# Unmasked decays in a hybrid SSD and attention block: the mask moves to the product of C and B, and the third pair's projections go between the convolution tiles

## The chip, the cores and the metric

The kernel runs on one core of a Trainium2 chip, in fp32 throughout (a matmul operand is split into a high and a low part, and three matmuls make one product). The metric is the device time of one execution, the median of several runs, in microseconds (us). Five engines take part, each with its own queue of instructions that it works through in order: PE (TensorE), DVE (VectorE), ACT (ScalarE), POOL (GpSimd) and SP (SyncE, which issues most DMAs here).

## The reference, cut to what matters

The block mixes a Mamba-2 SSD group (8 heads) and a stick-breaking attention group (8 heads, in 4 pairs), joins them by an output projection with normalization, and adds a gated feed-forward part. The change touches the SSD group and the order of the projections:

```python
proj = h @ w_in                                  # z, xbc, dt_raw, q, k, v
xbc = silu(causal_depthwise_conv(xbc, conv_w, conv_b))   # x, B and C of the SSD
a_cs = cumsum(dt * a)                            # per head
decay_in = exp(segsum(adt))                      # exp(a_cs[l] - a_cs[s]) where l >= s, else 0
cb = einsum("bclgn,bcsgn->bgcls", cc, bc)        # C times B, per group of 4 heads
y_diag = einsum("bgcls,bgrcls,bcsgrp->bclgrp", cb, decay_in, x)
```

Only the product of `cb`, `decay_in` and the mask counts, so the mask may stand on any factor. `a` is negative, so the difference is at most 0 wherever the mask keeps it.

## The kernel before, in words

The sequence of 1024 is cut into 8 blocks of 128. The front of the kernel normalizes and splits the input and projects q, k and v of the first pair of heads (q0, k0, v0). `dt_stage` then computes the time steps and their running sum `acs`, writes it to DRAM, and reads it back broadcast to all partitions, one tile `ab` (128 x 8 heads x 128, 512 KB) for each block. For each block it masks `ab` on POOL (an affine_select that puts -1e30 above the diagonal, L360), subtracts `acs` on DVE (one tensor_tensor over 8 heads, L361), takes the exponential on ACT (L362), and stores the decays to DRAM by a DMA that POOL issues (L363). The tiles `ab` borrow the buffers of the attention (`sp`, `sn`) and of the SSD (`u`, `dec`). Behind the last exponential ACT makes the scales `msc` that the attention's sigmoids need.

Then two streams are woven into one by `merge`. One is the attention: for each unit of a pair, a head and a query block, `weigh` makes scores on PE (`zp`, L565 and L566), two sigmoids on ACT (`sn` L567, `sp` L568), a select on POOL (L570), a running product on DVE (the scan, L571) and a product (L572); `turn` transposes the weights on PE (`tp`, L582) and splits them (`wh` on ACT, `wl` on DVE, L587); `mix_v` multiplies by v (`o`, L594). The other is the filling work, in the order of the table `PLAN`: `qkv1` (projections of the second pair), `x0` to `x7` (projections of xbc with their convolutions, whose taps on DVE, L384, are taken up as side work), `qkv2`, the SSD, `qkv3`, and the gates `z0` to `z3`. Every projection is made in two halves of 512 columns (`pj_q`, `pj_k`, `pj_v`, `pj_x`: 24 matmuls each, L78 to L80) in two PSUM banks, and each half is read out by DVE (`kr` L278, `vr` L284, `u` L375) before its bank can be used again. `merge` counts the PE time that the filling has issued and the DVE time that the attention has issued, and lets the attention go on while its share is below a curve through the nine values of `PACE`; so the table `PACE` sets when the attention starts and how fast it goes beside the filling. What comes out is one fixed order for each engine.

In the SSD, `front` makes for one block the products of C and B on PE (`pcb`, L420), multiplies them into the decays that are read back from DRAM (`Gm`, L427), and `ssd` multiplies `Gm` by the inputs on PE (`py`, L445). A front is issued one step ahead of the `py` that uses it.

After the last gate come the output projection and the feed-forward part, which is more than half of the time.

Of the kernel before, what the change touches and what calls it, by code (L numbers as in the profile page):

```python
# [33 lines left out]
NEG = -1e30  # L34

PLAN = ('qkv1', 'x0', 'x1', 'x2', 'x3', 'x4', 'x5', 'qkv2', 'x7', 'x6', 'ssd', 'qkv3', 'z0', 'z1', 'r0', 'z2', 'z3', 'wo', 'l1', 'o0')

PACE = (-0.109, 0.104, 0.264, 0.337, 0.474, 0.601, 0.751, 0.876, 1.027)
# [10 lines left out]
def tile_hybrid_block(  # L49
# [126 lines left out]
    ORDER = [f"{k}{t[3]}" if t[:3] == "qkv" else t for t in PLAN if t[0] in "qxz" for k in ("qkv" if t[0] == "q" else "x")]  # L176
# [83 lines left out]
    def qkv_tiles(j, st):  # L260
# [15 lines left out]
        def evac_k(n, ps, sl):  # L276
            kr = t2.tile([P, 512], F32, tag="t2", name="kr")
            V.tensor_tensor(kr, ps, R_b[:, sl], ALU.mult)  # L278
            two("k", n, kr)
            st["k"] = n == 1  # L280
# [13 lines left out]
    v_first = []  # L294

    def proj_qkv(j, st):
        for key, evac in zip("qkv", qkv_tiles(j, st)):
            yield from proj(f"{key}{j}", evac, {"q": 0.6, "k": 1.2, "v": 0.6}[key])


    def dt_stage():
# [50 lines left out]
        yield  # L352
        for b in range(NB):
# [6 lines left out]
            G.affine_select(ab, ab, [[0, NH], [-1, P]], ALU.is_ge, NEG, base=0, channel_multiplier=1)  # L360
            V.tensor_tensor(ab, ab, acs[:, b, :, None].to_broadcast([P, NH, P]), ALU.subtract)  # L361
            last = A.activation(ab, ab, AF.Exp)  # L362
            G.dma_start(dec_d[b], ab.rearrange("p h l -> p (h l)"))  # L363

        with tc.issue_after(last.ins):
            A.activation(rqp, rs, AF.Copy, scale=0.125)
            A.activation(rqn, rs, AF.Copy, scale=-0.125)

# [40 lines left out]
    def ssd():  # L409
        state = None  # L410

        def front(b):
# [8 lines left out]
            for g in range(2):  # L421
                T.transpose(pcb[:, 2 + g, :], cx[:, 4 + g, :], ident)
            bs = sml.tile([P, 2, P], F32, tag="bs", name="bs", bufs=2)
            A.copy(bs, pcb[:, 2:4, :])
            Gm = big.tile([P, NH, P], F32, tag="G", name="Gm")
            for g in range(2):
                V.tensor_tensor(  # L427
                    Gm[:, 4 * g : 4 * g + 4, :], de[:, 4 * g : 4 * g + 4, :],
                    pcb[:, g, None, :].to_broadcast([P, 4, P]), ALU.mult,
                )  # L430
# [173 lines left out]
    def attention(st):  # L604
# [6 lines left out]
        def ready(j):  # L611
            while "v" not in st[j]:
                yield 0, 0
# [92 lines left out]
    for _ in dts:  # L706
        pass
# [99 lines left out]
    def stage(t):  # L807
        nonlocal wo
        if t[:3] == "qkv":
            yield from proj_qkv(int(t[3]), st[int(t[3])])  # L810
        elif t[0] == "x":
# [609 lines left out]
```

## Time and profile before

| | |
|---|---|
| time, median of 3 runs | 1226.1 us (1224.39 to 1229.47) |
| time of the profiled execution | 1223.84 us |
| span of the profiled execution, first to last instruction | 1222.1 us |
| PE busy | 1186.1 us, 97% of the span |
| DVE busy | 929.8 us, 76% |
| ACT busy | 585.3 us, 48% |
| POOL busy | 92.6 us, 8% |
| mean granted clock of PE | 0.997 of full speed |

A row of the timeline gives the start, the duration, the engine, the line, the operation, what is written and read, the shapes and a count; behind it in brackets stand the engine's idle time before it and what ended that time. Rows of one line that follow each other are merged under one count. On PE and DVE an instruction begins before the one ahead of it has quite ended, so that the distance of two starts, and not a duration, is what an instruction costs in a dense stretch. In a table by stages the busy time of each engine stands with the number of its instructions behind it; what is missing to the length of the stage is idle time.

### The profile page before, as it was taken

The page shows a single profiled execution, that of the slowest core. Times are in us where ns is not written, and L with a number is a line of the kernel's source. Part 1 is how long each engine was busy: PE and PEld are TensorE (multiplying, and loading weights), DVE is VectorE, ACT ScalarE, POOL GpSimd, SP SyncE. Part 2 cuts the span into 40 slices and gives each one's busy share as a digit, 9 for nine tenths or more (in the row PEclk, how much of TensorE's full clock was granted, in tenths as well). Part 3 has the DMA queues.
Part 4 walks back from the last instruction along what each step waited for, and adds up shares of the span by engine and source line. Part 5 has one row for each costly group of instructions (what it writes and reads, how often), then busy time and mean ns, then how long its engine had stood idle before and what let it go on. Part 6 is the DMA issues. An engine that isn't in the chain of part 4 may idle for free.

```text
span 1222.1 us, 16315 instructions
## 1 busy us (share of the span) xinstructions
PE 1186.1 (97%) x5641; PEld 966.0 (79%) x5641; DVE 929.8 (76%) x1461; ACT 585.3 (48%) x1115; POOL 92.6 (8%) x232
## 2 busy tenths in 40 slices
PE   9998999999999998999999999999999999999997
PEld 7776778887887776788788888888888888888885
DVE  7478988769997978668898755566555558998877
ACT  7347655546654776446653323333233335444453
POOL 0041110010100100011200000000000000000000
PEclk9999999999999999999999999999999999999999
DMA  6793342345657424767973322322223298233346
GB/s 192 198 341 111 92 134 91 118 118 172 180 151 221 137 79 155 227 191 221 314 207 110 104 77 79 104 69 87 78 78 104 96 334 285 69 122 100 114 136 236
DMA packets 141994, 184.27 MB, mean 151 GB/s; under 512 B 10724, under 2 KB 96964, under 8 KB 141912
## 3 DMA queue, kind: packets, MB, share of 16 engines
q1 hardware_dynamic: 130656, 152.23, 40.8%
q0 software_dynamic: 7424, 25.17, 5.5%
q10 hardware_dynamic: 3832, 5.84, 1.3%
q8 instruction: 44, 0.72, 0.3%
q14 instruction: 38, 0.31, 0.1%
HBM read 133.28 MB, written 49.92 MB: 150 GB/s over the span
## 4 chain that ended last, share of the span: by engine, by line
PE 72%; DVE 13%; DMA 5%; ACT 5%; issue 4%; SPq 1%; DVEq 0%; ACTq 0%
PE pd L79 5%; PE pd L78 5%; PE pd L80 5%; DVE sn L571 3%; DMA Rb<-r_d 2%; PE o L594 2%; PE tp L582 2%; PE pj_x L78 2%; PE pj_x L80 2%; PE pcu L80 2%; PE pcg L80 2%; PE peu L80 2%; PE peg L80 2%; PE peu L79 2%; PE peg L79 2%
## 5 line engine op out<-in xcount | busy, mean ns | idle before, releaser
L74 ACT CAST flhi<-fraw 128x512 fp32r<-128x512 f32 x98 | 60.3, 621 | 153.5 <-PE pcg L79 35.6
L79 PE MATMUL pd<-folo,fohi 128*128 128x512 f32 x260 | 101.4, 390 | 0.0
L80 PE MATMUL pd<-fohi,folo 128*128 128x512 f32 x260 | 101.2, 389 | 0.0
L78 PE MATMUL pd<-fohi 128*128 128x512 f32 x260 | 101.2, 389 | 0.0
L571 DVE TENSOR_TENSOR_SCAN sn<-sn,smask 128x1024 f32<-128x1024 f32 (+3 forms) x64 | 87.3, 1365 | 17.6 <-ACT sn L567 17.4
L75 DVE TENSOR_TENSOR fllo<-fraw,flhi 128x512 fp32r<-128x512 f32 x98 | 66.7, 684 | 29.2 <-ACT flhi L74 29.2
L567 ACT ACTIVATE sn<-zp,msc 128x512 f32<-128x512 f32 (+2 forms) x96 | 56.0, 585 | 34.5 <-PE zp L566 28.9
L74 ACT CAST fohi<-rt 128x512 fp32r<-128x512 f32 x83 | 48.5, 618 | 45.6 <-PE pd L79 22.9
L586 ACT CAST wh<-tp 128x512 fp32r<-128x512 f32 (+1 forms) x80 | 42.7, 544 | 38.5 <-PE tp L582 38.0
L74 ACT CAST flhi<-fs 128x512 fp32r<-128x512 f32 x44 | 27.3, 622 | 69.5 <-PE peg L79 34.5
L75 DVE TENSOR_TENSOR folo<-rt,fohi 128x512 fp32r<-128x512 f32 x83 | 54.9, 687 | 7.3 <-ACT fohi L74 7.3
L587 DVE TENSOR_TENSOR wl<-tp,wh 128x512 fp32r<-128x512 f32 (+1 forms) x80 | 49.7, 628 | 10.8 <-ACT wh L586 10.3
L79 PEld LDWEIGHTS pd<-folo,fohi 128*128 128x128 f32 x260 | 48.8, 188 | 10.6 <-DVE folo L75 0.6
L568 ACT ACTIVATE sp<-zp,msc 128x512 f32<-128x512 f32 (+2 forms) x96 | 55.9, 585 | 2.5 <-PE tp L582 2.4
L78 PEld LDWEIGHTS pd<-fohi 128*128 128x128 f32 x260 | 48.8, 188 | 10.2
L80 PEld LDWEIGHTS pd<-fohi,folo 128*128 128x128 f32 x260 | 48.8, 188 | 10.1
L582 PE MATMUL tp<-ident,sp 128*128 128x128 f32 x288 | 48.0, 278 | 5.7 <-DVE sp L572 5.1
L78 PE MATMUL po<-woh,yhl 128*128 128x512 f32 x128 | 50.5, 395 | 2.6 <-ACT yhl L74 2.2
L1015 POOL DMA_DIRECT2D a_d<-sg x44 | 23.9, 542 | 376.8 <-DVE sg L1014 376.8
L78 PE MATMUL pj_x<-hh,wh_x 128*128 128x512 f32 x128 | 52.2, 408 | 0.0
L80 PE MATMUL pj_x<-hh,wl_x 128*128 128x512 f32 x128 | 51.0, 398 | 0.0
L80 PE MATMUL po<-woh,yhl 128*128 128x512 f32 x128 | 50.1, 393 | 0.5 <-DVE yhl L75 0.5
(425 smaller groups left out, 3457.6 us busy)
## 6 DMA issues: line engine op xcount, KB each, us to landing
ps<-a_d SPq DMA_DIRECT2D x55, 256.0 KB
fraw<-in_w_gate_dram SPq DMA_DIRECT2D x22, 512.0 KB
fraw<-in_w_up_dram SPq DMA_DIRECT2D x22, 512.0 KB
a_d<-sg POOLq DMA_DIRECT2D x44, 256.0 KB, 2.6
rt<-in_w_down_dram SPq DMA_DIRECT2D x33, 256.0 KB
rt<-a_d SPq DMA_DIRECT2D x22, 256.0 KB
ps<-in_w_down_dram SPq DMA_DIRECT2D x22, 256.0 KB
xt<-in_x_t_dram SPq DMA_DIRECT2D x8, 512.0 KB
```

The source lines that it names most:

```text
L74: A.copy(hi, src)
L75: V.tensor_tensor(lo, src, f32(hi), ALU.subtract)
L78: T.matmul(ps, lhsT=ah, rhs=bh, start=start, stop=False, skip_group_check=more)
L79: T.matmul(ps, lhsT=ah, rhs=bl, start=False, stop=False, skip_group_check=more)
L80: last_mm[0] = T.matmul(ps, lhsT=al, rhs=bh, start=False, stop=stop, skip_group_check=more)
L567: A.activation(sn[:, 1 + off : 1 + off + cw_], zp[:, 0:cw_], AF.Sigmoid, scale=rqn[:, qb : qb + 1])
L568: A.activation(sp[:, off : off + cw_], zp[:, 0:cw_], AF.Sigmoid, scale=rqp[:, qb : qb + 1])
L571: V.tensor_tensor_scan(sn[:, 1 : 1 + W], sn[:, 1 : 1 + W], smask[:, 0:W], 1.0, ALU.mult, ALU.max)
L582: T.transpose(tp[:, P * i : P * i + P], ws[a][:, co : co + P], ident)
L586: A.copy(wh[:, 0:n_], tp[:, 0:n_])
L587: V.tensor_tensor(wl[:, 0:n_], tp[:, 0:n_], f32(wh[:, 0:n_]), ALU.subtract)
L594: T.matmul(o[:, 0:cw_], lhsT=vv[:, k, h, :], rhs=wt[:, c0 : c0 + cw_], start=(first and k == kb + 1 and wt is wh), stop=(last and k == kb ...
```

## The change

The decays lose their mask: the affine_select on `ab` goes, and DVE subtracts `acs` with 64 tensor_scalar instructions (one for each block and head, 128 columns, subtract and then a minimum with 0) where 8 tensor_tensor instructions (1024 columns) stood. The mask is put on C times B instead: ACT copies the 256 columns of `pcb` to SBUF (`cb`), POOL masks them by an affine_select, and DVE multiplies the decays by `cb` rather than by PSUM.

The work on the 8 blocks is no longer issued in one piece ahead of the two streams. All 8 loads are still issued first; the rest becomes side work of the filling, one block at a time: three blocks at once, four after DVE has been given the first half of k1, and the last after the second half. The attention may begin its first unit only when all of this has been issued.

In `PLAN` the one entry `qkv2` becomes `q2`, `k2` and `v2` between x tiles, and the first five values of `PACE` are lower.

```diff
-PLAN = ('qkv1', 'x0', 'x1', 'x2', 'x3', 'x4', 'x5', 'qkv2', 'x7', 'x6', 'ssd', 'qkv3', 'z0', 'z1', 'r0', 'z2', 'z3', 'wo', 'l1', 'o0')
-PACE = (-0.109, 0.104, 0.264, 0.337, 0.474, 0.601, 0.751, 0.876, 1.027)
+PLAN = ('qkv1', 'x0', 'q2', 'x1', 'x2', 'k2', 'x3', 'x4', 'v2', 'x5', 'x7', 'x6', 'ssd', 'qkv3', 'z0', 'z1', 'r0', 'z2', 'z3', 'wo', 'l1', 'o0')
+PACE = (-0.14, 0.06, 0.195, 0.33, 0.465, 0.601, 0.751, 0.876, 1.027)
...
         def evac_k(n, ps, sl):
             kr = t2.tile([P, 512], F32, tag="t2", name="kr")
-            V.tensor_tensor(kr, ps, R_b[:, sl], ALU.mult)
+            i = V.tensor_tensor(kr, ps, R_b[:, sl], ALU.mult)
+            if j == 1:
+                k_evac.append(i)
...
+        abs_ = []
         for b in range(NB):
...
-            G.affine_select(ab, ab, [[0, NH], [-1, P]], ALU.is_ge, NEG, base=0, channel_multiplier=1)
-            V.tensor_tensor(ab, ab, acs[:, b, :, None].to_broadcast([P, NH, P]), ALU.subtract)
+            abs_.append(ab)
+        for b, ab in enumerate(abs_):
+
+            while len(k_evac) < (0, 1, 2)[(b > 2) + (b > 6)]:
+                yield 0, 0
+
+            with tc.issue_after(k_evac[-1].ins) if k_evac else nullcontext():
+                for h in range(NH):
+                    V.tensor_scalar(ab[:, h, :], ab[:, h, :], acs[:, b, h : h + 1], 0.0, ALU.subtract, ALU.min)
             last = A.activation(ab, ab, AF.Exp)
             G.dma_start(dec_d[b], ab.rearrange("p h l -> p (h l)"))
+            yield 0, 1.7
...
+        decayed.append(True)
...
+            cb = sml.tile([P, 2, P], F32, tag="cb", name="cb")
+            A.copy(cb, pcb[:, 0:2, :])
+            G.affine_select(cb, cb, [[0, 2], [-1, P]], ALU.is_ge, 0.0, base=0, channel_multiplier=1)
...
                 V.tensor_tensor(
                     Gm[:, 4 * g : 4 * g + 4, :], de[:, 4 * g : 4 * g + 4, :],
-                    pcb[:, g, None, :].to_broadcast([P, 4, P]), ALU.mult,
+                    cb[:, g, None, :].to_broadcast([P, 4, P]), ALU.mult,
                 )
...
-            while "v" not in st[j]:
+            while "v" not in st[j] or not decayed:
                 yield 0, 0
...
-    for _ in dts:
-        pass
+    for _ in range(4):
+        next(dts)
+    side.append(dts)
```

The order on DVE at the decays, before. `ab` is the tile of one block's decays, `kr` and `kl` belong to the second pair's k, whose two halves stand in the PSUM tiles `pj_k`; `ql` and `wl_v` are low parts of q1 and of the weights of v1, and `vv` is the first pair's v.

```order
L75 TENSOR_TENSOR wl_v_827<-wr_v_824,wh_v_826 128x512
L361 TENSOR_TENSOR ab<-ab,acs 128x1024
L75 TENSOR_TENSOR ql<-pj_q_768,qh 128x512
L361 TENSOR_TENSOR ab<-ab,acs 128x1024 x2
L278 TENSOR_TENSOR kr<-pj_k_799,R_b 128x512
L75 TENSOR_TENSOR kl<-kr,kh 128x512
L361 TENSOR_TENSOR ab<-ab,acs 128x1024 x4
L278 TENSOR_TENSOR kr<-pj_k_844,R_b 128x512
L550 TENSOR_TENSOR vv_925<-pv,vv_925 128x8x64
L75 TENSOR_TENSOR kl<-kr,kh 128x512
```

The same place on DVE after the change:

```order
L371 TENSOR_SCALAR ab<-ab,acs 128x128 x8
L74 TENSOR_TENSOR ql<-pj_q_748,qh 128x512
L371 TENSOR_SCALAR ab<-ab,acs 128x128 x16
L74 TENSOR_TENSOR wl_v_807<-wr_v_804,wh_v_806 128x512
L277 TENSOR_TENSOR kr<-pj_k_779,R_b 128x512
L371 TENSOR_SCALAR ab<-ab,acs 128x128 x4
L74 TENSOR_TENSOR kl<-kr,kh 128x512
L371 TENSOR_SCALAR ab<-ab,acs 128x128 x28
L277 TENSOR_TENSOR kr<-pj_k_834,R_b 128x512
L371 TENSOR_SCALAR ab<-ab,acs 128x128 x6
L74 TENSOR_TENSOR kl<-kr,kh 128x512
L371 TENSOR_SCALAR ab<-ab,acs 128x128 x2
```

Before, seven blocks stood ahead of the second half's `kr` and the eighth came some rows further down; now 56 of the 64 instructions stand ahead of it, and the last 8 right behind it.

The order on ACT between the last exponentials and the attention's first sigmoids, before. `wh_x` is the high part of the weights of x0, which a DMA loads.

```order
L362 ACTIVATE ab<-ab 128x1024
L74 CAST kh<-kr 128x512
L549 CAST vv_925<-pv 128x8x64
L74 CAST wh_x_949<-wr_x_947 128x512
L74 CAST wh_x_986<-wr_x_984 128x512
L362 ACTIVATE ab<-ab 128x1024
L366 ACTIVATE msc<-msc 128x8
L367 ACTIVATE msc<-msc 128x8
L567 ACT_TABLE_LOAD
L567 ACTIVATE sn<-zp,msc 128x512
L568 ACTIVATE sp<-zp,msc 128x512
```

And after:

```order
L372 ACTIVATE ab<-ab 128x1024 x4
L73 CAST kh<-kr 128x512
L73 CAST wh_x_924<-wr_x_922 128x512
L372 ACTIVATE ab<-ab 128x1024
L377 ACTIVATE msc<-msc 128x8
L378 ACTIVATE msc<-msc 128x8
L73 CAST wh_x_961<-wr_x_959 128x512
L582 ACT_TABLE_LOAD
L582 ACTIVATE sn<-zp,msc 128x512
L583 ACTIVATE sp<-zp,msc 128x512
```

One of the two casts of x0's weights still stands ahead of the last exponential, the other now behind it; the readout of `vv` has moved behind the first sigmoids.

The order on PE at the first block of the SSD (block 7), before. `pxs` are transposes of the inputs, `pj_k` belongs to the fourth pair.

```order
L422 MATMUL pcb<-ident,cx 128x128 x2
L433 MATMUL pxs<-ident,cx 128x128 x4
L582 MATMUL tp<-ident,sp 128x128 x4
L80 MATMUL pj_k_3244<-hh_0_187,wl_k_2967 128x512
L78 MATMUL pj_k_3244<-hh_0_189,wh_k_2966 128x512
L79 MATMUL pj_k_3244<-hl_0_190,wh_k_2966 128x512
L565 MATMUL zp<-kh,qq 128x512
L566 MATMUL zp<-kl,qq 128x512
L594 MATMUL o<-wh,vv_2898 128x256
L80 MATMUL pj_k_3244<-hh_0_189,wl_k_2967 128x512
L565 MATMUL zp<-kh,qq 128x384
L445 MATMUL py<-xdt,Gm 128x64 x8
```

And after:

```order
L434 MATMUL pcb<-ident,cx 128x128 x2
L448 MATMUL pxs<-ident,cx 128x128 x4
L597 MATMUL tp<-ident,sp 128x128 x8
L77 MATMUL pj_k_3282<-hh_0_195,wh_k_3011 128x512
L609 MATMUL o<-wh,vv_2937 128x256
L78 MATMUL pj_k_3282<-hl_0_196,wh_k_3011 128x512
L460 MATMUL py<-xdt,Gm 128x64 x4
L79 MATMUL pj_k_3282<-hh_0_195,wl_k_3012 128x512
L460 MATMUL py<-xdt,Gm 128x64 x4
```

The first `py` stands behind fewer matmuls than before, and there are now a copy and a select between `pcb` and the `Gm` that `py` reads.

Behind the gates z0 to z3 every engine has the same order as before.

## Rows read from the trace of the kernel before

**Rows 1.** The page's first part: busy time, share of the span and number of instructions of each engine.

```profile
PE 1186.1 (97%) x5641; PEld 966.0 (79%) x5641; DVE 929.8 (76%) x1461; ACT 585.3 (48%) x1115; POOL 92.6 (8%) x232
```

**Rows 2.** The table by stages: start and end of a stage, its length, then busy time and number of instructions of PE, weight loads, DVE, ACT and POOL, PE's granted clock, the DMA engines' busy share and GB/s.

```profile
85.60:94.40 8.80, 7.20 (x30) 5.28 (x29) 7.65 (x9) 4.77 (x8) 2.98 (x8) 1.00 1.02 365
94.40:110.00 15.60, 10.97 (x52) 8.43 (x53) 11.14 (x10) 12.65 (x25) 2.35 (x8) 0.89 0.32 100
110.00:150.00 40.00, 36.91 (x204) 30.25 (x203) 38.71 (x52) 27.17 (x51) 5.15 (x19) 1.00 0.36 93
150.00:200.00 50.00, 47.81 (x241) 38.45 (x240) 44.45 (x53) 27.68 (x47) 5.51 (x17) 1.00 0.40 116
200.00:250.00 50.00, 48.56 (x254) 40.96 (x254) 39.42 (x51) 27.71 (x51) 4.62 (x18) 1.00 0.39 118
250.00:300.00 50.00, 49.06 (x251) 39.33 (x250) 39.81 (x49) 29.96 (x54) 5.31 (x15) 1.00 0.42 120
300.00:405.00 105.00, 103.00 (x647) 87.26 (x648) 93.74 (x148) 58.35 (x134) 10.30 (x40) 1.00 0.62 184
```

**Rows 3.** Who PE waited for from 80 to 110 us: the waiting instruction, what ended the wait, us in total, times, the longest.

```profile
PE zp L565 <- ACT sp L568: 3.5, 1, 3.5
PE pj_v L78 <- DVE kr L278: 1.6, 1, 1.6
PE tp L582 <- DVE sp L572: 0.6, 1, 0.6
PE o L594 <- DVE wl L587: 0.5, 1, 0.5
```

**Rows 4.** The timeline of PE: two matmuls of k1 in a dense stretch, the transposes of the first pair's v, the two long waits, and two matmuls behind the second.

```profile
67.25 0.39 PE L78 MATMUL pj_k<-hh,wh_k 128*128 128x512 f32 x1
67.48 0.39 PE L79 MATMUL pj_k<-hl,wh_k 128*128 128x512 f32 x1
...
80.48 1.03 PE L548 MATMUL pv<-ident,vr 128*128 128x128 f32 x8
...
87.22 0.50 PE L78 MATMUL pj_v<-hh,wh_v 128*128 128x512 f32 x1 [1.58 <-DVE kr L278]
...
97.90 0.50 PE L565 MATMUL zp<-kh,qq 128*128 128x512 f32 x1 [3.52 <-ACT sp L568]
...
100.06 0.63 PE L78 MATMUL pj_x<-hh,wh_x 128*128 128x512 f32 x1
100.49 0.63 PE L79 MATMUL pj_x<-hl,wh_x 128*128 128x512 f32 x1
```

**Rows 5.** The timeline of DVE at the decays and at the attention's first weights.

```profile
75.24 0.68 DVE L278 TENSOR_TENSOR kr<-pj_k,R_b 128x512 f32<-128x512 f32 x1
76.95 5.07 DVE L75 TENSOR_TENSOR kl<-kr,kh 128x512 fp32r<-128x512 f32 x1 [1.03 <-ACT kh L74]
81.95 4.62 DVE L361 TENSOR_TENSOR ab<-ab,acs 128x1024 f32<-128x1024 f32 x4
86.49 0.68 DVE L278 TENSOR_TENSOR kr<-pj_k,R_b 128x512 f32<-128x512 f32 x1
...
92.77 1.21 DVE L361 TENSOR_TENSOR ab<-ab,acs 128x1024 f32<-128x1024 f32 x1
...
100.96 1.22 DVE L572 TENSOR_TENSOR sp<-sp,sn 128x1024 f32<-128x1024 f32 x1 [0.20 <-POOL sp L570]
...
104.32 1.09 DVE L572 TENSOR_TENSOR sp<-sp,sn 128x896 f32<-128x896 f32 x1 [0.20 <-ACT sp L568]
```

**Rows 6.** The timeline of POOL at the decays.

```profile
77.25 4.22 POOL L360 TENSOR_SCALAR_AFFINE_SELECT ab<-ab 128x1024 f32<-128x1024 f32 x4
...
88.78 1.11 POOL L360 TENSOR_SCALAR_AFFINE_SELECT ab<-ab 128x1024 f32<-128x1024 f32 x1
```

**Rows 7.** The timeline of ACT from the casts of x0's weights to the first sigmoids.

```profile
88.84 1.15 ACT L74 CAST wh_x<-wr_x 128x512 fp32r<-128x512 f32 x2
94.01 1.06 ACT L362 ACTIVATE ab<-ab 128x1024 f32<-128x1024 f32 x1 [4.03 <-DVE ab L361]
...
95.28 1.28 ACT L567 ACT_TABLE_LOAD   x1
96.58 0.69 ACT L567 ACTIVATE sn<-zp,msc 128x512 f32<-128x512 f32 x1
97.17 0.68 ACT L568 ACTIVATE sp<-zp,msc 128x512 f32<-128x512 f32 x1
```

**Rows 8.** The timeline of SP: the issue of the two loads of x0's weights (start, us, count).

```profile
82.42 1.18 SPq L168 DMA_DIRECT2D wr_x<-in_w_in_dram  x2
```

**Rows 9.** Groups of DVE by line and shape (count, busy us, mean ns of one, idle us before): 128 columns of SBUF with two tensors, and with one tensor and two constants.

```profile
L755 DVE TENSOR_TENSOR rt<-rt 36x128 f32<-36x128 f32 x2 | 0.6, 283 | 0.2
...
L757 DVE TENSOR_SCALAR rt<-rt 36x128 f32<-36x128 f32 x2 | 0.4, 216 | 0.0
```

**Rows 10.** The copy of the second half of `pcb` on ACT, as a group of the same kind.

```profile
L424 ACT COPY bs<-pcb 128x256 f32<-128x256 f32 x8 | 3.0, 378 | 3.2 <-PE pcb L422 3.2
```

**Rows 11.** Selects of 128 columns on POOL, as groups of the same kind: the attention's, and one at the kernel's start.

```profile
L570 POOL TENSOR_SCALAR_AFFINE_SELECT sp<-sp 128x128 f32<-128x128 f32 x64 | 32.0, 501 | 182.2 <-ACT sp L568 180.9 <-PE zp L565 1.1
...
L111 POOL TENSOR_SCALAR_AFFINE_SELECT tri<-ones_f 128x128 f32<-128x128 f32 x1 | 0.3, 290 | 0.0
```

**Rows 12.** The view of line 363, the stores of the decays that POOL issues: from issue to landing, us.

```profile
DMA to landing us min/median/max: 4.2/5.2/7.7
```

More of the change, by code (lines that the diff above doesn't have):

```diff
@@ L33 @@
 EPS = 1e-6
-NEG = -1e30
-PLAN = ('qkv1', 'x0', 'x1', 'x2', 'x3', 'x4', 'x5', 'qkv2', 'x7', 'x6', 'ssd', 'qkv3', 'z0', 'z1', 'r0', 'z2', 'z3', 'wo', 'l1', 'o0')
-PACE = (-0.109, 0.104, 0.264, 0.337, 0.474, 0.601, 0.751, 0.876, 1.027)
+PLAN = ('qkv1', 'x0', 'q2', 'x1', 'x2', 'k2', 'x3', 'x4', 'v2', 'x5', 'x7', 'x6', 'ssd', 'qkv3', 'z0', 'z1', 'r0', 'z2', 'z3', 'wo', 'l1', 'o0')
+PACE = (-0.14, 0.06, 0.195, 0.33, 0.465, 0.601, 0.751, 0.876, 1.027)
 A_ALL, F_ALL = 146.4, 259.0
@@ L172, in load_w_half @@
         return hi, lo
-    ORDER = [f"{k}{t[3]}" if t[:3] == "qkv" else t for t in PLAN if t[0] in "qxz" for k in ("qkv" if t[0] == "q" else "x")]
+    ORDER = [f"{k}{t[3]}" if t[:3] == "qkv" else t for t in PLAN if t[0] in "qkvxz" for k in ("qkv" if t[:3] == "qkv" else "x")]
     START = {"q": COL_Q, "k": COL_K, "v": COL_V, "x": COL_XBC, "z": COL_Z}
@@ L292, in qkv_tiles, with proj_qkv @@
         return evac_q, evac_k, evac_v
-    v_first = []
-    def proj_qkv(j, st):
+    v_first, k_evac, decayed = [], [], []
+    def proj_qkv(j, st, keys="qkv"):
         for key, evac in zip("qkv", qkv_tiles(j, st)):
-            yield from proj(f"{key}{j}", evac, {"q": 0.6, "k": 1.2, "v": 0.6}[key])
+            if key in keys:
+                yield from proj(f"{key}{j}", evac, {"q": 0.6, "k": 1.2, "v": 0.6}[key])
     def dt_stage():
@@ L810, in stage @@
             yield from proj_qkv(int(t[3]), st[int(t[3])])
+        elif t[0] in "qkv":
+            yield from proj_qkv(int(t[1]), st[int(t[1])], t[0])
         elif t[0] == "x":
```

## The prediction

> **What bounds the kernel now.** I read the page's first part, then the table by stages, then who PE waited for in the stage where it stood still longest, then the timelines of the engines that it waited for. PE is busy for 97% of the span [rows 1], so an edit is worth the time in which PE waits because of it, and nothing beyond that. Behind the gates the order of every engine stays, so what is won or lost is settled between the decays and the gates. The stages show where there is something to win [rows 2]: PE stands still for 1.60 us from 85.6 to 94.4 us and for 4.63 us from 94.4 to 110, and in the second of these its granted clock is 0.89. From 110 to 200 us it is idle for 3.09 + 2.19 = 5.28 us while DVE is busy for 83.16 of 90 us (92%); from 200 to 300 us for 1.44 + 0.94 = 2.38 us while DVE is busy for 79.23 of 100 (79%).
>
> Four waits make the idle time of 80 to 110 us [rows 3]. The long ones are 1.58 us for a PSUM bank of k1 that DVE had not read out (`kr`), and 3.52 us for a score bank that ACT's first sigmoids had not read out [rows 4]. Behind the second, matmuls of 512 columns come 0.43 us apart instead of 0.23 [rows 4]: the lower of PE's two clocks, 1.2 instead of 2.4 GHz. Over that stage it costs (1 - 0.89) x 15.6 = 1.7 us [rows 2]. Behind the wait of 1.58 us the granted clock stayed at 1.00 [rows 2].
>
> Both long waits come from the decays. DVE's `kl` took 5.07 us [rows 5], where the next subtraction of twice its size takes 1.21, and it covers POOL's four selects, 4.22 us from 77.25 [rows 6]: DVE was held while POOL masked. Four subtractions follow (4.62 us), and only then `kr` at 86.49 [rows 5]. The eighth block's select comes at 88.78 [rows 6], its subtraction at 92.77 [rows 5], its exponential at 94.01, then the load of a table and the first sigmoids, which end at 97.85 [rows 7]; PE goes on at 97.90 [rows 4].
>
> **The change part by part.**
>
> *The selects on POOL go.* That frees DVE of some 5.07 - 0.68 = 4.4 us of being held at `kl` (the 0.68 is `kr`, of the same size) and takes a step out of the chain of each block.
>
> *64 small subtractions for 8 large ones.* The nearest row is a tensor_scalar of 128 columns, 216 ns, against 283 for a tensor_tensor of that size [rows 9]. In a dense row an instruction costs less than its duration: four subtractions take 4.62 us, one alone 1.21, so the distance is (4.62 - 1.21) / 3 = 1.14, or 0.07 less. So 64 cost between 64 x 0.14 = 9.0 and 64 x 0.216 = 13.8 us, against 8 x 1.14 = 9.1 before. Alone that would be 0 to +4.7 us on DVE; with the 4.4 us of holding gone it is -4.5 to +0.3.
>
> *The wait for `kr`.* In the new order `kl` and 28 subtractions (3.9 to 6.0 us) stand between the two halves. With `kl` starting at 76.95 as before, the second `kr` starts at 81.5 to 83.7. PE wanted its bank at 87.22 - 1.58 = 85.64 [rows 4]. The wait goes, with 2 us to spare or more: -1.58.
>
> *The wait for the sigmoids.* Behind `kr` come the last 8 subtractions and `kl`, 0.68 + 0.68 + 1.1 to 1.7 us: the last block is ready for its exponential at 84.0 to 86.8. On ACT a cast of x0's weights now stands ahead of that exponential. Their load was issued at 82.42 [rows 8] and cast at 88.84 [rows 7], so it takes 6.4 us at most in this crowded stage; it now stands behind `kl`'s store, can go out near 78, and is there by 84.4, so the cast is covered by DVE's end or nearly so. From the start of the exponential to the end of the first pair of sigmoids were 97.85 - 94.01 = 3.84 us; the other cast adds 0.6 [rows 7]: the score bank is free at 88.5 to 91.2. PE comes to that bank later in its order than before: the second half of v1 and 6 of the 8 transposes of the first pair's v stand ahead of it. It reaches v1's second half at 85.64 - 0.8 = 84.8 (the transposes, 1.03 us with the last one's tail, have moved behind), and then needs 12 x 0.227 + 0.7 = 3.4 us: 88.2. Wait: 0.3 to 3.0 us. I take 1.3, near the middle: -2.2.
>
> *What is late next.* The first weights need about 102.2 - 97.9 = 4.3 us from there to the end of their product on DVE, and the second ones 3.2 more (104.32 + 1.09) [rows 5]. In the new order, its matmuls counted and taken at the dense distance, PE has some 3.1 us of other work before the first transposes and some 2.2 before the second ones. That makes two waits of about 1 us, where 0.6 and 0.5 stood [rows 3]: +0.9, with 0.5 to 3.5 us of new waits as its ends (-0.6 to +2.4).
>
> *The clock.* If no wait is longer than 1.58 us, the granted clock stays at full as it did behind that one: -1.7. With a wait of 3 us it falls as before: 0.
>
> *q2, k2 and v2 between x tiles.* The x tiles carry the taps, so DVE's load is uneven [rows 2]: 92% with the tiles x0 to x4, 79% where q2, k2 and v2 stood. Mixed, it is 162.4 / 190 = 85%. PE's idle time was 0.059 us for each us in the first and 0.024 in the second. At the lower rate throughout, 7.7 us become 4.5: -3.1 at best. At the mean of both rates nothing is won; and PLAN and PACE reorder every engine, which may cost as much as 1 us. Waits pile up where an engine is almost full, so I take the value nearer to the better end: -2.0.
>
> *The mask in the SSD.* For each of 8 blocks ACT copies 256 columns (0.378 us by the same form [rows 10]) and POOL selects 256 columns: above the 0.29 us of one of 128 columns at the kernel's start, and near the mean of 0.50 of the attention's [rows 11]. No engine is full by that (ACT's 8 x 0.38 = 3 us in 105 us where it is busy for 58 [rows 2]). What counts is the chain from `pcb` to `py`: +0.9 us. In the order the first block has about 2 us of other matmuls to cover it, the later ones more than 4. So one block shows it: +0.5, ends 0 and +4.
>
> Sum: -1.58 - 2.2 + 0.9 - 1.7 - 2.0 + 0.5 = -6.1 us. The profiled execution took 1223.84 us (1.7 us outside its span); it would take 1217.7. It lies 2.3 us under the median of the runs, 1226.1, against which the forecast is made: **1220.0 us**.
>
> **The rivals.**
>
> *The wait moves and stays.* The cast ahead of the last exponential waits for its load, or the subtractions cost 216 ns each: PE waits 3 us at the score bank, the clock falls as before. Then -1.58 - 0.5 + 0.9 + 0 - 1.0 + 0.5 = -1.7: 1224.4. For it: DMA engines at a share of 1.02 [rows 2]. Against it: the load goes out 4 us earlier.
>
> *Everything comes out well.* No wait at the score bank, new waits of 0.5 us, the mix at its best: -1.58 - 3.5 - 0.6 - 1.7 - 3.1 + 0 = -10.5: 1215.6.
>
> *POOL's stores are held by DVE.* POOL was seen to hold DVE; the reverse, in the new form, no row shows. If each store can be issued only when an unbroken row of subtractions ends, the seventh block's goes out up to 1.7 us later, lands 5.2 us after that [rows 12], and a memset of POOL behind it holds the attention's first select. The first two waits at the weights grow by about 1 us each: -4.1, 1222.0. The Trainium skill, "SBUF — State Buffer", section "SBUF: two separate sides", says why it might: a DMA issued by GpSimd needs descriptors that GpSimd writes, and it cannot write them while DVE runs an operation that takes both ports, such as a one-tensor fp32 operation in SBUF. Before, DVE used two-tensor operations there and the stores landed in 4.2 to 7.7 us, so the trace does not decide it.
>
> *Slower: the mask in the SSD.* PE works in order, and `py` waits for `Gm`, which now waits for ACT, whose queue may hold 0.6 us of other work, and for POOL, which DVE can hold to about 0.6. With the copy that is 0.38 + 0.6 + 0.6 = 1.6 us for each block. If it shows on all 8, it costs 12.6 us against the 6.6 won elsewhere: +6.0, 1232.1. The sign turns at a little over 4 blocks exposed. For it: DVE is 89% busy in that stage [rows 2], and its queue holds `Gm`, so it waits too. Against it: the matmuls between `pcb` and `py` in the new order, from the second block on.
>
> **How the numbers follow.** Forecast 0.46, with its own range from 1217 to 1223; everything well 0.22; the wait moves 0.14; POOL's stores 0.06; the SSD 0.12. What a measurement can tell from no change is about 0.5%, 6.1 us here, so 1220.0 is the border. Faster: half of the forecast and all of "well", 0.45. Slower: the SSD, 0.12. Same: the rest, 0.43. The range takes the best case less 2 us and the moved wait plus the 3.4 us by which one run lay above the median: 1213 to 1228; it leaves out the SSD and a little below.
>
> **What would show it.** In the new profile: no row of DVE at the decays longer than 1.3 us, and tensor_scalar rows of 0.14 to 0.22 us; the second `kr` before 84 us and no wait of `pj_v` for it; the first sigmoid at 87 to 90 us instead of 96.58; a granted clock of 1.00 from 90 to 110 us; PE's idle time from 110 to 300 us under 6 us; no wait of `py` longer than 1 us but at the first block. The prediction is wrong if PE still waits over 2.5 us for a sigmoid, if the waits at the weights behind it come to over 3.5 us, if DVE falls behind in the mixed stretch, or if `py` waits at block after block.

## The result and the profile after

The changed kernel took 1228.62 us in the median of 20 runs, the kernel before 1226.18 us in 20 runs beside them: a ratio of 1.0022, with a 95% interval of 1.0012 to 1.0031. It is slower by about 2.4 us, where I had forecast 1220.0 us and a range of 1213 to 1228. One of the 20 executions took 4202 us and, like one each in experiments 4 and 5, is left out of the ratio, though not of the median. The profiled execution of after has a span of 1227.3 us, against 1222.1 before. These 5.2 us say little of the price of the change: the granted clock, averaged over a run, was 0.994 in the runs of both kernels, but 0.993 in the profile of after and 0.997 in that of before, which was one of its better ones. PE's idle time over the whole span is the same, 1227.3 - 1191.6 = 35.7 us after and 1222.1 - 1186.1 = 36.0 before; what differs is PE's busy time.

The page's first part, after, beside [rows 1]: PE is as full as before, and no engine has much more to do.

```profile
PE 1191.6 (97%) x5641; PEld 967.8 (79%) x5641; DVE 927.6 (76%) x1517; ACT 588.3 (48%) x1123; POOL 86.6 (7%) x232
```

The table by stages, after, with the columns of [rows 2]. PE's idle time (length less busy) is 4.41 us from 85.6 to 94.4, where it was 1.60, and 0.89 in the next stage, where it was 4.63. The clock is 0.97 and 0.91 there. From 110 to 300 us it is 6.47 us (before 7.65), but it has moved: 2.26 in the first 90 us (before 5.28) and 4.21 in the next 100 (before 2.38). From 300 to 405, where the SSD is, it is 3.56 (before 2.00). Together, from 85.6 to 405 us, it is about 0.5 us less than before.

```profile
85.60:94.40 8.80, 4.39 (x23) 3.48 (x22) 2.75 (x4) 6.38 (x11) 0.73 (x3) 0.97 1.06 378
94.40:110.00 15.60, 14.71 (x75) 12.02 (x74) 15.14 (x17) 9.84 (x20) 2.62 (x8) 0.91 0.37 110
110.00:150.00 40.00, 39.21 (x204) 32.20 (x204) 32.21 (x42) 22.42 (x42) 3.80 (x16) 1.00 0.41 112
150.00:200.00 50.00, 48.53 (x246) 38.21 (x245) 41.94 (x53) 30.77 (x55) 4.67 (x18) 1.00 0.43 126
200.00:250.00 50.00, 48.07 (x258) 40.15 (x257) 42.05 (x54) 28.14 (x50) 4.62 (x18) 1.00 0.36 95
250.00:300.00 50.00, 47.72 (x242) 37.66 (x242) 44.84 (x53) 31.30 (x55) 4.40 (x17) 1.00 0.41 111
300.00:405.00 105.00, 101.44 (x622) 83.30 (x621) 88.93 (x142) 58.05 (x138) 16.63 (x45) 1.00 0.60 176
```

Who PE waited for from 80 to 110 us, after, beside [rows 3]: the wait for `kr` is gone; the wait for the sigmoids is still there, and is longer.

```profile
PE zp L580 <- ACT sp L583: 4.4, 1, 4.4
PE o L609 <- DVE wl L602: 0.6, 1, 0.6
PE tp L597 <- DVE sp L587: 0.3, 1, 0.3
```

The timeline of DVE, after, beside [rows 5]: `kl` is back at 0.68 us, the second `kr` starts at 82.62 instead of 86.49, and the last subtraction ends at 85.47. A subtraction costs 5.59 / 28 = 0.20 us, so the 64 take 12.8 us.

```profile
76.53 0.68 DVE L74 TENSOR_TENSOR kl<-kr,kh 128x512 fp32r<-128x512 f32 x1
77.13 5.59 DVE L371 TENSOR_SCALAR ab<-ab,acs 128x128 f32<-128x128 f32 x28
82.62 0.68 DVE L277 TENSOR_TENSOR kr<-pj_k,R_b 128x512 f32<-128x512 f32 x1
...
85.00 0.47 DVE L371 TENSOR_SCALAR ab<-ab,acs 128x128 f32<-128x128 f32 x2
```

The timeline of ACT, after, beside [rows 7]: the last block is ready at 85.47, but its exponential starts at 87.51. The cast ahead of it waited 2.65 us for the load of x0's weights, and the second cast 1.01 us more. So the first sigmoid starts at 91.70.

```profile
86.98 0.62 ACT L73 CAST wh_x<-wr_x 128x512 fp32r<-128x512 f32 x1 [2.65 <-DMA wr_x<-in_w_in_dram]
87.51 1.05 ACT L372 ACTIVATE ab<-ab 128x1024 f32<-128x1024 f32 x1
...
89.77 0.62 ACT L73 CAST wh_x<-wr_x 128x512 fp32r<-128x512 f32 x1 [1.01 <-DMA wr_x<-in_w_in_dram]
90.40 1.28 ACT L582 ACT_TABLE_LOAD   x1
91.70 0.69 ACT L582 ACTIVATE sn<-zp,msc 128x512 f32<-128x512 f32 x1
```

The timeline of SP, after, beside [rows 8]: these loads were issued at 77.74, 4.7 us earlier than before, as I had worked out. The cast of the first starts 9.2 us behind the first issue.

```profile
77.74 1.92 SPq L167 DMA_DIRECT2D wr_x<-in_w_in_dram  x2
```

Behind the gates, where the order is the same, the output projection (`po`) waits for `yhl`, the high part of its input that ACT casts: the longest such wait is 3.3 us after and 1.4 before (the first row is after, the second before).

```profile
PE po L77 <- ACT yhl L73: 3.3, 1, 3.3
PE po L78 <- ACT yhl L74: 2.2, 2, 1.4
```

From 510 to 520 us, in the columns of [rows 2], PE has no idle time in either kernel, but 39 matmuls fall into this stage after, at a granted clock of 0.83, and 46 before, at 1.00. After, the clock also falls to 0.66 from 485 to 490 us, where it is 1.00 before.

```profile
510.00:520.00 10.00, 10.00 (x39) 8.05 (x38) 7.82 (x22) 6.38 (x21) 0.55 (x1) 0.83 0.75 223
510.00:520.00 10.00, 10.00 (x46) 8.29 (x45) 8.64 (x25) 4.89 (x18) 1.08 (x2) 1.00 0.71 215
```

The view of the DMA engines from 70 to 96 us, after, in 40 slices and as a sum: 26 us at 391 GB/s, the engines busy in every slice. POOL's queue (q0), which holds the stores of the decays, has 3.70 MB of it.

```profile
DMA  9999999999999999999999999999999999999999
...
DMA packets 5181, 10.17 MB, mean 391 GB/s; under 512 B 418, under 2 KB 2445, under 8 KB 5178
...
q0 software_dynamic: 1014, 3.70, 35.3%
```

The timeline of POOL, after, in place of [rows 6]: a store is issued in 0.5 to 0.8 us, but a memset of the attention's `sn` stands behind the third and waits 5.93 us until an earlier store has landed; four stores then go out in a row.

```profile
76.02 0.59 POOL L373 DMA_DIRECT2D dec_d<-ab  x1 [0.99 <-ACT ab L372]
82.55 0.10 POOL L574 MEMSET sn<- 128x1 f32 x1 [5.93 <-DMA dec_d<-ab]
83.03 2.16 POOL L373 DMA_DIRECT2D dec_d<-ab  x4 [0.39 <-issue]
```

The new select in the SSD, after, as the view of its line (duration least, median, most; first and last start), beside [rows 11], with what DVE waited for it, us and times. Its copy on ACT takes 0.374 us in the median.

```profile
L437 POOL TENSOR_SCALAR_AFFINE_SELECT cb<-cb x8: 408/408/1930, 309.0 to 402.7; 128x256 f32<-128x256 f32 x8
...
  DVE Gm L442: 1.0, 4
```

### The profile page after: what moved, and what is told of

It is laid out like the page before. It is cut to its first block, busy times and chain, and to the rows that moved or that the text cites. A ratio compares the mean times of both kernels' runs of the same rounds, so it can differ in the third digit from the quotient of the medians.

```text
span 1227.3 us, 16366 instructions
## 1 busy us (share of the span) xinstructions
PE 1191.6 (97%) x5641; PEld 967.8 (79%) x5641; DVE 927.6 (76%) x1517; ACT 588.3 (48%) x1123; POOL 86.6 (7%) x232
## 4 chain that ended last, share of the span: by engine, by line
PE 72%; DVE 11%; ACT 3%; issue 3%; DMA 3%; POOL 0%; SPq 0%; DVEq 0%; ACTq 0%; POOLq 0%
PE pd L79 5%; PE pd L77 5%; PE pd L78 5%; DVE sn L586 3%; PE po L77 2%; PE po L79 2%; PE po L78 2%; PE pj_x L77 2%; PE pj_x L79 2%; PE pj_x L78 2%; DVE sp L587 2%; PE pcg L78 2%; PE peu L78 2%; PE peg L78 2%; PE pcu L78 2%
## 5 line engine op out<-in xcount | busy, mean ns | idle before, releaser
L602 DVE TENSOR_TENSOR wl<-tp,wh 128x512 fp32r<-128x512 f32 (+1 forms) x80 | 49.7, 628 | 10.2 <-ACT wh L601 9.8
L78 PEld LDWEIGHTS pd<-folo,fohi 128*128 128x128 f32 x260 | 48.8, 188 | 10.2
L79 PEld LDWEIGHTS pd<-fohi,folo 128*128 128x128 f32 x260 | 48.8, 188 | 10.2
L597 PEld LDWEIGHTS tp<-ident,sp 128*128 128x128 f32 x288 | 33.5, 140 | 22.7 <-DVE sp L587 13.0
L587 DVE TENSOR_TENSOR sp<-sp,sn 128x1024 f32<-128x1024 f32 (+3 forms) x64 | 48.2, 754 | 4.2 <-POOL sp L585 1.5
```

The source lines that it names most:

```text
L78: T.matmul(ps, lhsT=ah, rhs=bl, start=False, stop=False, skip_group_check=more)
L79: last_mm[0] = T.matmul(ps, lhsT=al, rhs=bh, start=False, stop=stop, skip_group_check=more)
L587: V.tensor_tensor(sp[:, 0:W], sp[:, 0:W], sn[:, 0:W], ALU.mult)
L597: T.transpose(tp[:, P * i : P * i + P], ws[a][:, co : co + P], ident)
L602: V.tensor_tensor(wl[:, 0:n_], tp[:, 0:n_], f32(wh[:, 0:n_]), ALU.subtract)
```

## The experiments

Each was timed beside the kernel before on the same chip; "ratio" is to that kernel, with its 95% interval. Experiments 1 to 4, 5 to 8, 9 to 11 and 12 have each their own runs of it, with medians of 1226.35, 1225.86, 1225.71 and 1225.41 us, so between these groups I compare ratios; a difference of two ratios is known to about 2 us either way. Theory at the outset: the decays win what I said, but x0's load gives it back, and the mask in the SSD costs more than I said. Rivals: the tables cost it, or the clock.

**1. The change again.** No edit.

> The changed kernel once more, beside the next three on one chip. Expected by both theories: ratio to before 1.000 to 1.004 (1226 to 1231 us). Theory M (the wait moved): PE again waits 4 us or more for the first sigmoids at 88 to 93 us and its granted clock falls behind that wait; the clock falls at one or two more places in some executions, in the output projection above all, so that the mean granted clock is lower than before's (0.993 to 0.997). Rival N (noise of single executions): the mean clock of several runs is the same as before's and the ratio is 1.000.

1228.35 us, ratio 1.0018 (1.0007 to 1.0029), mean clock of the runs 0.994 for both kernels. The loss stands, and a run's mean clock does not explain it. Neither theory came out whole: PE's wait for the sigmoids was 3.4 us, under the 4 of M, and M's lower mean clock is not there; the ratio is not the 1.000 of N.

**2. The decays and the mask, with the old tables.**

```diff
-PLAN = ('qkv1', 'x0', 'q2', 'x1', 'x2', 'k2', ...
-PACE = (-0.14, 0.06, 0.195, 0.33, 0.465, ...
+PLAN = ('qkv1', 'x0', 'x1', 'x2', 'x3', 'x4', 'x5', 'qkv2', ...
+PACE = (-0.109, 0.104, 0.264, 0.337, 0.474, ...
```

> Only the decays and the mask are changed; PLAN and PACE are those of before. Theory M: the wait for kr is gone, the wait for the first sigmoids stays at 3 us or more, and the mix of 110 to 300 us is as uneven as before: 0.999 to 1.004. Rival P (the tables cost): the new tables give back what the decays win, so that the decays alone are faster: 0.995 or less (1220 us).

1228.62 us, ratio 1.0018 (1.0009 to 1.0028): the same as with the new tables. PE's wait for the sigmoids was 2.9 us, and its idle time from 110 to 300 us 6.4 us without any mixing. Rival P is out.

**3. The new tables on the old decays.** The kernel before with the new PLAN and PACE, and the entries `q2`, `k2`, `v2`.

> The kernel before with the new PLAN and PACE alone (masked decays in one piece, DVE's 8 large subtractions). Theory M: PE's idle time from 110 to 300 us is within 1.5 us of before's 7.7, since DVE's work is shifted and not made less: 0.998 to 1.003. Rival P: 1.003 or more. If mixing the tiles does win 2 us as the prediction had it: 0.998.

1231.36 us, ratio 1.0045 (1.0033 to 1.0057). Its waits at the start were longer than those of before: 5.1 us for the sigmoids and 2.4 for `kr`. PE's idle time from 110 to 300 us was 7.3 us, 0.4 under before's. So the tables alone cost 5 us, as rival P has it, and with the new decays nothing. The `kr` wait, which the new decays remove, is one place where the two meet; that it makes up the 5 us is not shown.

**4. No mask.** The copy and the select are left out and DVE reads `pcb` from PSUM, so nothing masks the decays at all.

```diff
-            A.copy(cb, pcb[:, 0:2, :])
-            G.affine_select(cb, cb, ...
...
-                    cb[:, g, None, :].to_broadcast([P, 4, P]), ALU.mult,
+                    pcb[:, g, None, :].to_broadcast([P, 4, P]), ALU.mult,
```

> The changed kernel without the copy of C times B to SBUF and without its select: the product is read from PSUM as before, and the mask is left out altogether. If the mask's way over ACT and POOL costs what the stage from 300 to 405 us shows (PE's idle time 3.6 us against 2.0 before): 1.3 to 2.5 us less than the changed kernel, a ratio to before of about 1.000. If it costs the 0.5 us of the prediction: within 0.7 us of the changed kernel. If the rival of the prediction holds (every block exposed): 6 us less or more.

1226.4 us, ratio 1.0002 (0.999 to 1.0014): the mask costs 1228.4 - 1226.4 = 2.0 us, known to about 2 us either way. PE's idle time from 300 to 405 us was 2.42 us (3.50 in experiment 1).

**5. The mask on DVE.**

```diff
-            A.copy(cb, pcb[:, 0:2, :])
-            G.affine_select(cb, cb, ...
+            V.tensor_tensor(cb, pcb[:, 0:2, :], tri[:, None, :].to_broadcast([P, 2, P]), ALU.mult)
```

> The mask over C times B is applied by one product of 256 columns on DVE (PSUM times the triangle of ones that stands in SBUF) instead of a copy on ACT and a select on POOL; all else is the changed kernel. Theory A (the price of the mask is the chain over two more engines, ACT then POOL, each waited for): the select's 0.4 to 1.9 us go, PE's idle time from 300 to 405 us falls from 3.6 to under 2.8 us, the time to 1226.5-1227.5 us (ratio 1.000 to 1.001). Theory B (the mask costs where DVE is nearly full, so 8 more products of about 0.35 us on it cost what the chain did or more): 1228.5 us or above (ratio 1.002 or more).

1228.32 us, ratio 1.0014 (1.0000 to 1.0027): neither theory is told apart by the time. The stage, in the columns of [rows 2], speaks for A: PE is idle for 105.00 - 102.94 = 2.06 us. One execution is weak evidence for it: with the same mask on DVE the stage has 2.3 us in experiments 7 and 11, but 4.0 in experiment 8 and 3.4 in experiment 12.

```profile
300.00:405.00 105.00, 102.94 (x637) 86.23 (x636) 91.85 (x151) 56.74 (x132) 12.42 (x37) 1.00 0.59 176
```

PE's wait for the sigmoids was long in this execution, in the view of its waits, though at 1225.80 us the execution was one of the faster ones:

```profile
PE zp L579 <- ACT sp L582: 6.6, 1, 6.6
```

The start of the kernel is the same program in experiments 1, 4 and 5 as in the changed kernel, and the wait for the sigmoids was 3.4, 7.2, 6.6 and 4.4 us: what is waited for is a load, and its time varies from one execution to the next. These four executions took 1228.39, 1228.44, 1225.80 and 1229.06 us, so the length of this wait alone does not settle the time of an execution.

**6. x0's casts behind the first sigmoids.** The loads stay; the split is traced later.

```diff
-        split(hi, lo, raw)
+        if name == "x0":
+            x0_split.append((hi, lo, raw))
+        else:
+            split(hi, lo, raw)
...
+            with tc.issue_after(i.ins):
+                while x0_split:
+                    split(*x0_split.pop(0))
```

(`i` is the second sigmoid of a score bank.)

> The loads of x0's weights stay where they are, but their split into two parts (ACT's cast and DVE's difference) is queued behind the first two sigmoids, so the last exponential no longer stands behind a cast that waits for its load. Theory A (the wait for the sigmoids is that cast's load, nothing else): the last exponential starts within 0.3 us of DVE's last subtraction, the first sigmoids at 88 to 89.5 instead of 91.7 us, PE's wait for them falls from 3.4 - 4.4 to under 1 us, its granted clock there stays at 1.00, and the time is 1223.5 to 1225.5 us (ratio 0.998 to 0.9995). Theory B (the wait only moves: the first weights' select stands behind a memset that waits for a store of the decays, and x0's split comes late for PE): waits of tp for the first weights or of pj_x for wh_x of 2 us or more, time 1227 to 1229.

1226.05 us, ratio 0.9998 (0.9985 to 1.0012): by the ratios 2.5 us less than experiment 1, a little less than A said. The exponential starts as DVE ends, and the first sigmoid at 87.36 (timeline of ACT):

```profile
84.79 1.06 ACT L377 ACTIVATE ab<-ab 128x1024 f32<-128x1024 f32 x1 [1.18 <-DVE ab L376]
...
87.36 0.69 ACT L587 ACTIVATE sn<-zp,msc 128x512 f32<-128x512 f32 x1
```

Who PE waited for from 80 to 112 us in this kernel: the wait for the sigmoids is down to 1.5 us, but 3.1 us at the first weights (`tp`) have come up behind it. Its granted clock was 1.00 from 85.6 to 110 us. Both theories hold a part.

```profile
PE tp L605 <- DVE sp L595: 3.1, 2, 2.4
PE zp L585 <- ACT sp L588: 1.5, 1, 1.5
```

**7. All together, new tables.** Experiments 5 and 6, and the memset of `u` traced at its tile's second half.

> Both of the above, and the memset of the three columns behind x0's tile is traced later, so that on POOL it no longer stands ahead of the first select and waits there for a store of the decays; with the new PLAN and PACE. Theory A (three separate prices: wait for the sigmoids 3 to 5 us with the clock, mask 1 us, memset 1 us): 1222 to 1224 us (ratio 0.9965 to 0.998). Theory B (from 110 us on DVE sets the pace, and what PE wins at the start it waits for again behind): 1225 to 1227.5, with PE's idle time from 110 to 300 us above 8 us.

1223.45 us, ratio 0.9976 (0.9964 to 0.9987): theory A. It is faster than both kernels, 2.4 us under the kernel before. From 85.6 to 110 us PE is idle for 3.67 us at a clock of 1.00. Its runs' mean clock was 0.996, against 0.994 beside it. How much of the gain is the clock's stays open: the two profiled executions, both at a mean clock of 0.997, differ by 2.4 us in span as well, and 2.2 of that is PE's idle time (33.8 us, before 36.0).

**8. The same with the old tables.**

> As the one before, with the old PLAN and PACE. The decays alone with the old tables took as long as the whole change (1228.6 both). If the tables are worth nothing with the new decays, this run lies within 1 us of the one before; if mixing q2, k2, v2 between the x tiles is worth the 2 us forecast, it lies 1.5 to 3 us above it; if the tables cost, as they did with the old decays (5 us), it lies below it.

1222.72 us, ratio 0.9972 (0.996 to 0.9983): within 1 us of experiment 7. No worth of the tables shows.

**9. Eight large operations for the 64 small ones**, in the changed kernel.

```diff
-                for h in range(NH):
-                    V.tensor_scalar(ab[:, h, :], ab[:, h, :], acs[:, b, h : h + 1], 0.0, ALU.subtract, ALU.min)
+                V.tensor_tensor(ab, ab, acs[:, b, :, None].to_broadcast([P, NH, P]), ALU.min)
```

> The changed kernel with one operation for each block of the decays instead of eight: a minimum of two tensors over 1024 columns (the size and the place of the subtraction of before, and free of selects). The decays come out as the minimum of the two sums instead of their clipped difference, so that part of the computation is changed; the time of all else is not. Theory A (x0's load, not DVE, sets the last exponential): DVE is done with the last block 2.5 to 4 us earlier (about 82 us instead of 85.5), but the cast ahead of the exponential still waits for its load to 86 us or later, PE's wait for the sigmoids stays at 2.5 us or more, and the time at 1227 to 1229 us (ratio 1.001 to 1.0025). Theory B (the 64 small subtractions, at 0.20 us each instead of the least I had allowed, 0.14, set it): the wait falls under 1.5 us, the time to 1224 to 1226 us (ratio 0.9985 to 1.000).

1231.34 us, ratio 1.0046 (1.0034 to 1.0058). DVE was done by 80.13 us, over 5 us earlier than in the changed kernel, and the last exponential ended at 82.25; the time rose by 3 us. But more than DVE had changed. The scheduler had put x0's first cast between the sigmoids, and the loads of x0's weights were issued at 83.06 instead of 77.74, behind the store of the second `kl`. The cast came 9.4 us behind its load's issue, where the changed kernel has 9.2; ACT stood there for 6.82 us, PE for 6.5 (timeline of ACT):

```profile
84.92 0.69 ACT L581 ACTIVATE sn<-zp,msc 128x512 f32<-128x512 f32 x1
92.43 0.62 ACT L73 CAST wh_x<-wr_x 128x512 fp32r<-128x512 f32 x1 [6.82 <-DMA wr_x<-in_w_in_dram]
92.95 0.68 ACT L582 ACTIVATE sp<-zp,msc 128x512 f32<-128x512 f32 x1
```

Theory B's gain did not come: with DVE done early, the wait was still the load's. As the load went out 5.3 us later too, this run does not say what a faster DVE alone would be worth.

**10. Half of each store.**

```diff
-            G.dma_start(dec_d[b], ab.rearrange("p h l -> p (h l)"))
+            G.dma_start(dec_d[b][:, 0:512], ab.rearrange("p h l -> p (h l)")[:, 0:512])
...
```

> The changed kernel, in which POOL stores only the first half of each block of the decays (256 KB instead of 512) and the SSD loads that half twice, so half of the decays are wrong and 2 MB less are written between 74 and 96 us. Theory A (x0's load comes late because the DMA engines are full in that stretch, 10.2 MB from 70 to 96 us at about 390 GB/s, and the stores take 35% of them): the cast's wait of 2.65 us falls under 1 us, PE's wait for the sigmoids under 2.5 us, the first select comes before 92.5 us, and the time falls by 2 to 4 us, to 1224.5 to 1226.5. Theory B (x0's load waits in its own queue, behind the loads and stores that SP issued ahead of it, and the stores from POOL's queue do not matter): waits as in the changed kernel, 1227.5 to 1229.

1225.38 us, ratio 0.9999 (0.9987 to 1.0012): by the ratios 2.3 us less than experiment 1. With 8.68 MB instead of 10.17 from 70 to 96 us, the first cast waits 1.52 us instead of 2.65 and the second not at all, and PE's wait for the sigmoids is 2.1 us. Theory A, though not all of it: the first select came at 94.41, hardly earlier than the 94.70 of the changed kernel, as a memset ahead of it waits for a store. The DMA view of this kernel from 70 to 96 us:

```profile
DMA packets 4867, 8.68 MB, mean 334 GB/s; under 512 B 449, under 2 KB 2497, under 8 KB 4864
```

And its PE's wait:

```profile
PE zp L581 <- ACT sp L584: 2.1, 1, 2.1
```

**11. The new PLAN with the old PACE**, else as experiment 7.

> The kernel with the new tables that took 1223.45 us (mask on DVE, x0's split behind the first sigmoids, memset later), with the new PLAN but the old PACE: q2, k2, v2 between the x tiles at the old rate of the attention. Theory A (mixing is worth something and the new PACE, which holds the attention back at the start, gives it away): 1220 to 1222 us (ratio 0.995 to 0.997), PE idle from 110 to 300 us under 5.5 us. Theory B (mixing is worth nothing: PE's idle time there depends on DVE's total work, 161 to 162 us of 190 in all four kernels, not on its order): 1222.5 to 1224.5, PE idle there 6 to 7.5 us as with either pair of tables.

1222.96 us, ratio 0.9981 (0.997 to 0.9991); PE idle for 6.6 us from 110 to 300: theory B. With 6.5 us in both experiments 7 and 8, the order of the tiles does not matter there.

**12. POOL's stores ahead of its memsets**, else as experiment 7: `with tc.issue_after(stores[-1].ins):` around the memsets of `sn` and `u`.

> The kernel with the new tables that took 1223.45 us, with POOL's memsets of sn and of x0's three columns queued behind the last of the eight stores of the decays. In all kernels with the new decays a memset stands among the stores and waits 3 to 6 us until an earlier store has landed, and the stores behind it are issued in a row when it is done. Theory A (POOL's own memsets hold the stores, and through them the first select): the fourth to eighth store are issued by 87 us, each right behind its exponential, the first select comes 1 to 3 us earlier than 91.3 us, PE's waits of tp fall from 1.8 to under 1 us, the time to 1221.5 to 1223 us (ratio 0.996 to 0.9975). Theory B (the DMA engines are full anyway, so earlier stores only take the place of the loads of x0's weights and of the first head): x0's casts wait by as much as is won, the sum of PE's idle time from 85.6 to 110 us stays at 3.5 us or more, the time at 1223 to 1225.

1225.84 us, ratio 0.9999 (0.9989 to 1.0009), 2.4 us more than experiment 7: theory B, and a little slower than it said. The stores do go out behind their exponentials, and the first select comes at 89.05 instead of 91.34. But x0's first cast, which did not wait in experiment 7, now stands for 2.33 us among the sigmoids, and PE waits 3.5 us there. The timelines of POOL, DVE and ACT in this kernel:

```profile
78.45 0.57 POOL L378 DMA_DIRECT2D dec_d<-ab  x1 [2.78 <-ACT ab L377]
80.02 0.57 POOL L378 DMA_DIRECT2D dec_d<-ab  x1 [1.00 <-ACT ab L377]
```

```profile
76.19 5.58 DVE L376 TENSOR_SCALAR ab<-ab,acs 128x128 f32<-128x128 f32 x28
```

```profile
90.73 0.62 ACT L73 CAST wh_x<-wr_x 128x512 fp32r<-128x512 f32 x1 [2.33 <-DMA wr_x<-in_w_in_dram]
```

## Why the prediction was wrong, step by step

*What the parts cost.* By the medians of experiments 1 to 4, which share their runs of the kernel before (1226.35 us): the mask 2.0 us (experiment 1 less 4), the tables -0.3 (1 less 2), and so the decays 2.3 - 2.0 = 0.3 us (experiment 2 less the kernel before, less the mask). I had forecast +0.5, -2.0 and -4.6. The intervals are about 0.1% either way, 1.3 us, and a difference of two is known to about 2 us. So the signs of the two small ones stay open, and the 0.5 of the mask lies near the edge of what the runs allow; that the decays won 4.6 us is out, and the 2.0 of the tables show in no pair of runs (experiment 7 less 8 is +0.7).

*The step that failed: x0's load.* I took the 6.4 us between the issue at 82.42 and the cast at 88.84 as the most that this load needs, so that an earlier issue would land by 84.4. That was a bound for an issue at 82.42 only. The load now went out at 77.74 and was cast at 86.98, 9.2 us later: an issue 4.7 us earlier brought the cast 1.9 us earlier. From 76 to 90 us the DMA engines moved 365 GB/s before and 403 after. In experiment 10, with 1.5 MB less to move, the same load was cast 8.2 us behind its issue, so the bytes that it shares the engines with count. In the changed kernel the last block is ready 2 us before its exponential, which stands behind this load; with the cast out of the way (experiment 6) the exponential starts as DVE ends, and with fewer bytes (experiment 10) the wait is 2.1 us. So this load, and not DVE, sets the sigmoids: a wait of 3.4 to 4.4 us, and up to 7.2 in experiments 4 and 5, in place of 1.3, where [rows 3] has 3.5. With it the term of the clock fell (0.91 where I had 1.00), as the prediction's condition of 3 us said. The rival "the wait moves and stays" named this mechanism; I gave it too little because I had priced the load from one row. It put the time at 1224.4; the mask's other 1.5 us, and the 1.0 that it still gave the tables, bring it to 1226.9, which leaves 1.7 us to the 1228.6 measured.

*What was taken as nothing: the rest of the kernel.* The prediction settled everything between the decays and the gates, since the order behind them is the same. But from 85.6 to 405 us PE's idle time changed by -0.9 - 1.2 + 1.6 = -0.5 us in the profiles, where the runs say +2.4. Behind the gates the profile of after has a longer wait of `po` for `yhl`, 3.3 us against 1.4, and a fall of the clock behind it, both shown above. The longest such wait was 3.3 and 3.8 us in experiments 1 and 2 and 1.7 to 2.9 in experiments 3 to 12. No experiment was made on that stretch, and the runs' mean clock is the same for both kernels: whether the change brings this wait, and what it costs in the median, stays open.

*The wait for `kr`: right.* It went, the second `kr` at 82.62. In experiment 3, where the decays are the old ones, it stayed and was 2.4 us.

*The small subtractions: near the upper end*, 0.20 us in a dense row where I allowed 0.14 to 0.216. It did not decide the time of the last exponential, for which the block was ready 2 us early.

*What is late next.* +0.9 was forecast, and the profile after has 0.9 us of such waits where 1.1 stood. That is no success: behind a long wait for the sigmoids the weights have time. Where that wait was short, in experiment 6, the waits at the weights were 3.1 us for `tp` and 0.4 for `wl`, 2.4 above the 1.1 of [rows 3] and so at my upper end.

*Mixing q2, k2, v2: wrong.* I let PE's idle time follow the lower of two rates. It fell by 3.0 us where DVE's load became lighter and rose by 1.8 where it became heavier, and from 110 to 300 us the changed kernel and experiments 2, 7, 8 and 11 have 6.4 to 6.6 us with either order (experiment 1 has 7.5). What one part won by a lighter load the other lost. The 1.2 us by which the sum fell are there without mixing in experiment 2, and mixing on the old decays (experiment 3) gave 0.4. That the sum follows DVE's work instead, 162.4 us before and 161.0 after, is not shown: experiment 12 has less of it, 159.6 us, and 7.7 us of idle time, and one program run twice differs by 1.0 us (6.5 and 7.5).

*The mask: mis-sized*, 2.0 us for 0.5. The prediction's two hops are there: DVE waited for the select in 4 blocks, and one select took 1.93 us where the median is 0.41. PE shows hardly a wait with the mask's name; its idle time in the stage rose by 1.56 us in small pieces. That the price went there through DVE's queue is likely but not shown. The signal I had promised, a wait of `py` over 1 us, was the wrong one to look for.

*POOL's stores held by DVE: no.* In experiment 12 two stores were issued in 0.57 us each, at 78.45 and 80.02, beside an unbroken row of DVE's subtractions from 76.19 to 81.77; they landed in 7.6 and 7.4 us, as the other six did in 7.2 to 8.6. The rule of the Trainium skill, "SBUF — State Buffer", section "SBUF: two separate sides", is that a DVE operation on both ports keeps GpSimd from writing its descriptors; nothing of it can be measured here, and no run shows whether these subtractions take both ports. What did hold the stores was POOL's own queue, by a memset.

*Open.* Three things are not known. The granted clock was 0.94 from 30 to 60 us in 6 of the 12 profiled executions of kernels with changed decays, and 1.00 in the others and in both with the old ones; PE is idle for 0.1 us in that stage, so no wait there explains it, and at 0.06 x 30 it costs about 1.8 us where it happens. Experiment 5 gained little beside experiment 4, though its wait at the start, 6.6 us, is not longer than the 7.2 there. And it is not shown whether the falls of the clock behind the gates belong to the change.

## What to carry to other kernels

Where the DMA engines were full, the time from the load's issue to its first cast was no property of the load: 6.4 us at most before, 8.4 to 10.2 in the four executions of one program, 14.1 in experiment 12. So price an earlier issue by the bytes that must pass, and keep an instruction that waits for such a load out of the way of a chain that PE waits for. Moving the cast won about 2.5 us with no work removed. And compare idle time over all stages that an order touches: a stall that leaves one stage may only have been moved to the next. Add up the terms of the profile at the end as well: here they come to -0.5 us where the runs say +2.4, which shows that a part of the time lies where nobody had looked.

## What the runs showed that I had not expected

The same program, started the same way, waited from 3.4 to 7.2 us at the same place (the changed kernel and experiments 1, 4 and 5). So the price of a wait for a load in this full stretch is wide, and one profile does not give it.

Issuing stores sooner made the kernel slower (experiment 12, 2.4 us). Up to the SSD the two kernels differ in POOL's order alone; that the cast waits in the one and not in the other suggests that the blocked queue had let x0's load pass.
